# Two weight tiles trade slots, gate tiles alternate between two rings, and 17 instead of 15 gate/up tiles go by block products, in a hybrid decoder layer on one Trainium2 core

## Chip, cores and metric

The kernel runs on one core of a Trainium2 chip. The metric is the device time of the whole program in microseconds (us), lower is better. In the profile PE is TensorE's matmul and PEld its weight load, DVE is VectorE, ACT is ScalarE, POOL is GpSimd, SP is SyncE, which here only issues DMAs.

## What is computed

One decoder layer over 512 tokens of width 1024, cut from the reference:

```python
u = rms_norm(x, pre_mix_w)
proj = einsum('btd,de->bte', u, w_in)       # hg_q hg_f hg_i hg_g dn_q dn_k dn_v dn_g dn_a dn_b m_a m_b
o_a = head_rms_norm(hgrn2_mix(hg_q, hg_f, hg_i, lb)) * silu(hg_g)          # gated linear recurrence
o_b = head_rms_norm(gated_deltanet_mix(conv(dn_q, dn_k, dn_v), ...)) * silu(dn_g)
merged = sigmoid(m_a) * (o_a @ w_o_hg) + sigmoid(m_b) * (o_b @ w_o_dn)
h = x + rms_norm(merged @ w_out, post_mix_w)
gate, up = split(rms_norm(h, pre_ffn_w) @ w_gate_up)                        # 2 x 2816 columns
out = h + rms_norm((silu(gate) * up) @ w_down, post_ffn_w)
```

## The kernel before

Features lie on the 128 partitions and tokens in the free dimension. Every large product is made from three products of a high and a low part (`mm3`, lines 124 to 127): high by high (L126), low by high (L126), high by low (L127). `wload` (L109 to L122) brings a weight tile in with a DMA on SP's queue, makes its high part on ACT (L118) and its low part on DVE (L119). `dense_in` computes 128 output features of an input projection (called a dense tile here): 24 matmuls with 512 columns into one of three PSUM banks called `mm`, and then a function that empties the bank.

The order of the program's text is not the order on the engines: a scheduler places every instruction when the program is built. `high_priority` moves instructions ahead, `issue_after` holds one behind another, and a tile of a ring (a tag with so many buffers) can only be placed when the ring has a free buffer, in the order in which the program asks for them. On each engine the instructions then run in the built order. Three rings matter here: `dct` (9 buffers, L70), `hct` (7 buffers) and `out` (1 buffer, `spill`, L76).

Around the change the program does this:

- The DeltaNet mixer runs chunk by chunk (4 chunks of 128 tokens). While it runs, dense tiles fill TensorE.
- The sigmoid gates of the merge (`m_a`, `m_b`) that are computed early go out to DRAM. `gate_out` takes an `out` tile, applies the sigmoid with three ACT passes (L151 to L153), and issues a DMA on ACT's queue to `early_b` or `early_a`. It is used for the four tiles of `m_b0`, the four of `m_a0` and the first of `m_a1`. The program's text asks for the last two (the fourth of `m_a0` and the first of `m_a1`) just ahead of the HGRN2 mixer.
- The HGRN2 mixer (`hg_attn`, `hg_step`, `head_norm`) works on 4 chunks. For each chunk there are column sums, which need `dct` tiles that ACT and DVE split into two parts, six levels of a decay matrix on `hct` tiles (DVE, ACT, DVE, PE, DVE), and a step of the recurrent state. The dense tiles for `hg_g` (its last two), the DeltaNet output projection `y0`, `m_b1`, the fourth of `m_a0` and the first of `m_a1` lie ahead of it in the text. Their matmuls are listed in `dense`, and the mixer's matmuls are held behind every fifth of them (`self.marks`, `paced`). A mark is a lower bound only: it does not make a matmul run right behind it.
- Then `m_a1`'s other three tiles, the HGRN2 output projection `y1` (`merge`, 96 matmuls), and `out_proj`. The 16 half tiles of `w_out` come in through `dct` tiles and are split on ACT and on DVE or POOL (POOL for every odd `i`). Tiles 6 and 7 go to slots 13 and 6, in which until then the gates `self.ma[1]` and `self.ma[0]` lie.
- In `ffn` there are 22 gate/up tiles. A direct one costs 48 matmuls with 512 columns. The others go by block products (`winograd`): 7 products of 12 matmuls with 256 columns (L1109 to L1111), with more work on DVE and ACT for the weight combinations. Tiles 0 to 2 and each with `ft % 4 == 2` are direct.

## Time and profile before

| | us |
|---|---|
| three timed runs | 811.60, 815.22, 814.64 (median 814.64) |
| the profiled execution, its own time | 811.25 |
| its span, first to last instruction | 809.5 |

| engine | busy, share of the span |
|---|---|
| PE | 796.2 us, 98% |
| DVE | 591.7 us, 73% |
| ACT | 489.3 us, 60% |
| POOL | 75.4 us, 9% |

The profiled execution is 0.4% below the median of the timed runs. TensorE's granted clock was at its upper level for nearly the whole span (mean 0.999). Busy time of PE counts matmuls that overlap, so a busy PE says that PE had something in hand, not that it ran at its peak.

### The profile page before, as it was taken

The page shows a single profiled execution, that of the slowest core. Times are in us where ns is not written, and L with a number is a line of the kernel's source. Part 1 is how long each engine was busy: PE and PEld are TensorE (multiplying, and loading weights), DVE is VectorE, ACT ScalarE, POOL GpSimd, SP SyncE. Part 2 cuts the span into 40 slices and gives each one's busy share as a digit, 9 for nine tenths or more (in the row PEclk, how much of TensorE's full clock was granted, in tenths as well). Part 3 has the DMA queues.
Part 4 walks back from the last instruction along what each step waited for, and adds up shares of the span by engine and source line. Part 5 has one row for each costly group of instructions (what it writes and reads, how often), then busy time and mean ns, then how long its engine had stood idle before and what let it go on. Part 6 is the DMA issues. An engine that isn't in the chain of part 4 may idle for free.

```text
span 809.5 us, 12379 instructions
## 1 busy us (share of the span) xinstructions
PE 796.2 (98%) x4713; PEld 682.6 (84%) x4713; DVE 591.7 (73%) x961; ACT 489.3 (60%) x924; POOL 75.4 (9%) x113
## 2 busy tenths in 40 slices
PE   8999999999999999999999999999999999999996
PEld 8988888876888788888878899999999998888885
DVE  4794998513676888985775698887988888757773
ACT  6748888635687656657534454555556557556552
POOL 1000048610002000001310000000000000000000
PEclk9999999999999999999999999999999999999999
DMA  8525252552216212147621311414141416656731
GB/s 305 188 84 205 82 156 79 137 182 79 78 49 221 82 53 79 40 130 240 229 91 40 130 53 53 157 53 157 53 156 53 157 53 224 219 185 208 252 109 53
DMA packets 37852, 104.30 MB, mean 129 GB/s; under 512 B 4512, under 2 KB 4928, under 8 KB 37664
## 3 DMA queue, kind: packets, MB, share of 16 engines
q1 hardware_dynamic: 32688, 89.18, 32.7%
q0 software_dynamic: 3232, 10.93, 5.1%
q10 hardware_dynamic: 1872, 3.41, 1.2%
q8 instruction: 37, 0.61, 0.3%
q14 instruction: 23, 0.19, 0.1%
HBM read 94.83 MB, written 8.66 MB: 128 GB/s over the span
## 4 chain that ended last, share of the span: by engine, by line
PE 87%; DVE 4%; ACT 4%; DMA 3%; issue 1%; DVEq 0%; ACTq 0%; POOLq 0%
PE mm L126 23%; PE mm L127 11%; PE hps L126 3%; PE hps L1109 2%; PE hps L1110 2%; PE hps L1111 2%; PE dps L1226 2%; DVE s L156 2%; PE mm L1226 2%; PE mm L1225 2%; PE mm L1224 2%; PE dps L1224 2%; PE dps L1225 2%; DMA early_a<-out 2%; PE hps L699 2%; PE dps L1110 2%
## 5 line engine op out<-in xcount | busy, mean ns | idle before, releaser
L126 PE MATMUL mm<-s,whi 128*128 128x512 f32 (+1 forms) x976 | 304.1, 390 | 0.0
L126 PEld LDWEIGHTS mm<-s,whi 128*128 128x128 f32 x976 | 177.0, 188 | 32.9 <-ACT s L130 0.2
L127 PE MATMUL mm<-s,wlo 128*128 128x512 f32 (+1 forms) x488 | 188.5, 386 | 0.0
L119 DVE TENSOR_TENSOR wlo<-raw,whi 128x1024 fp32r<-128x1024 f32 x66 | 84.2, 1278 | 59.3 <-ACT whi L118 58.6
L127 PEld LDWEIGHTS mm<-s,wlo 128*128 128x128 f32 x488 | 91.7, 188 | 17.4 <-DVE wlo L119 0.6
L118 ACT CAST whi<-raw 128x1024 fp32r<-128x1024 f32 x66 | 69.2, 1049 | 40.8 <-PE mm L126 30.1
L119 DVE TENSOR_TENSOR wlo<-s,whi 128x1024 fp32r<-128x1024 f32 x40 | 48.9, 1223 | 15.0 <-ACT whi L118 14.6
L130 ACT CAST whi<-raw 128x512 fp32r<-128x512 f32 x60 | 36.8, 618 | 25.0 <-PE dps L1110 7.0
L1109 PE MATMUL hps<-s,whi 128*128 128x256 f32 x180 | 50.0, 278 | 0.7 <-DVE hct L156 0.4
L1111 PE MATMUL hps<-s,wlo 128*128 128x256 f32 x180 | 49.7, 276 | 0.0
L1110 PE MATMUL hps<-s,whi 128*128 128x256 f32 x180 | 49.7, 276 | 0.0
L130 ACT CAST whi<-s 128x512 fp32r<-128x512 f32 x45 | 27.9, 619 | 35.1 <-PE hps L1110 13.9
L156 DVE TENSOR_TENSOR s<-s,s 128x512 fp32r<-128x512 f32 (+3 forms) x59 | 43.0, 743 | 4.0 <-ACT s L130 1.9
L1214 ACT CAST hct<-s 128x256 fp32r<-128x256 f32 x44 | 17.6, 406 | 41.9 <-PE mm L1226 26.2
L118 ACT CAST whi<-s 128x1024 fp32r<-128x1024 f32 x40 | 41.9, 1048 | 1.4 <-PE dps L1110 1.4
L156 DVE TENSOR_TENSOR wlo<-raw,whi 128x512 fp32r<-128x512 f32 x60 | 40.5, 684 | 0.5 <-ACT whi L130 0.2
L130 ACT CAST s<-s 128x512 fp32r<-128x512 f32 (+2 forms) x36 | 23.7, 667 | 26.9 <-DVE s L156 20.0
L156 POOL TENSOR_TENSOR s<-s 128x126 f32<-128x126 f32 (+22 forms) x62 | 35.1, 565 | 9.9 <-DMA s<-scr 5.2
L126 PE MATMUL hps<-s,whi 128*128 128x512 f32 (+1 forms) x128 | 35.4, 363 | 0.0
L1109 PEld LDWEIGHTS hps<-s,whi 128*128 128x128 f32 x180 | 33.8, 188 | 1.4 <-DVE hct L156 0.7
L1110 PEld LDWEIGHTS hps<-s,whi 128*128 128x128 f32 x180 | 33.8, 188 | 0.1
L1111 PEld LDWEIGHTS hps<-s,wlo 128*128 128x128 f32 x180 | 33.8, 188 | 0.0
(313 smaller groups left out, 1868.4 us busy)
## 6 DMA issues: line engine op xcount, KB each, us to landing
raw<-in_w_in_a_dram SPq DMA_DIRECT2D x44, 512.0 KB, 3.4
s<-in_w_down_dram SPq DMA_DIRECT2D x44, 512.0 KB, 4.6
s<-in_w_gu_dram SPq DMA_DIRECT2D x60, 256.0 KB, 3.8
raw<-in_w_gu_dram SPq DMA_DIRECT2D x14, 512.0 KB, 3.4
raw<-in_w_o_dram SPq DMA_DIRECT2D x8, 512.0 KB, 4.8
dct<-in_w_out_dram SPq DMA_DIRECT2D x16, 256.0 KB, 6.9
s<-in_w_iab_dram SPq DMA_DIRECT2D x8, 260.0 KB, 6.5
s<-in_xT_dram SPq DMA_DIRECT2D x8, 256.0 KB, 6.8
```

The source lines that it names most:

```text
L118: nc.scalar.copy(hi[:, :n], raw[:, :n])
L119: nc.vector.tensor_tensor(out=lo[:, :n], in0=raw[:, :n], in1=hi[:, :n].bitcast(F32), op=ALU.subtract)
L126: return [mm(ps, lh, rh, start=start, stop=False), mm(ps, lh, rl, start=False, stop=False), mm(ps, ll, rh, start=False, stop=stop)]
L127: mm(ps, ll, rh, start=False, stop=stop)]
L130: self.nc.scalar.copy(hi, src)
L156: return (eng or self.nc.vector).tensor_tensor(out=out, in0=a, in1=b, op=op)
L1109: mm(ps, wh[:, k, :], ah[k], start=start and k == 0, stop=False, skip_group_check=True)
L1110: mm(ps, wh[:, k, :], al[k], start=False, stop=False, skip_group_check=True)
L1111: mm(ps, wl[:, k, :], ah[k], start=False, stop=k == 3, skip_group_check=True)
L1224: T.matmul(ps[:, n], gh, w[0][:, cols], start=st, stop=False, skip_group_check=True)
L1225: T.matmul(ps[:, n], gh, w[1][:, cols], start=False, stop=False, skip_group_check=True)
L1226: T.matmul(ps[:, n], gl, w[0][:, cols], start=False, stop=sp, skip_group_check=True)
```

## The change

Three edits. In `out_proj`, tile 6 of `w_out` goes to slot 6 and tile 7 to slot 13. In `mixers`, from the third tile of `m_b0` on `gate_out` gets its tiles by turns from `out` and from `dct`: the third tile of `m_b0` from `out`, its fourth from `dct`, the tiles of `m_a0` from `out`, `dct`, `out` and (its fourth) `dct`, and the first of `m_a1` from `out`. In `ffn`, the direct tiles are 0, 1, 2, 9 and 16 instead of 0, 1, 2, 6, 10, 14 and 18, so that 17 instead of 15 go by block products, in runs of six, six and five.

```diff
--- before.py
+++ after.py
@@ -1,4 +1,5 @@
 import math
+from itertools import cycle
 from contextlib import ExitStack, contextmanager, nullcontext
 
 import numpy as np
@@ -812,9 +813,9 @@
             self.stt(t, ps, self.hnw, t, ALU.mult, ALU.mult)
             nc.sync.dma_start(out=early_g[i], in_=t)
 
-        def gate_out(to):
+        def gate_out(to, tiles=self.spill):
             def f(ft, ps):
-                t = self.spill()
+                t = tiles()
                 self.sigmoid(t, ps)
                 A.dma_start(out=to[ft], in_=t)
             return f
@@ -841,8 +842,10 @@
             self.hg_prep((2, 3))
             early_e = {lev: self.hg_decay(0, lev) for lev in HG_LEVELS[:5]}
 
-        self.dense_in("m_b0", gate_out(early_b), fts=range(2, 4))
-        self.dense_in("m_a0", gate_out(early_a), fts=range(3))
+        two = cycle((self.spill, lambda: self.dct((P, 512))))
+        tiles = lambda: next(two)()
+        self.dense_in("m_b0", gate_out(early_b, tiles), fts=range(2, 4))
+        self.dense_in("m_a0", gate_out(early_a, tiles), fts=range(3))
         self.hq = self.slot(11, [P, NC_, NH, P])
         self.ghg = self.slot(12, [P, NH, S])
         for c in range(NC_):
@@ -868,8 +871,8 @@
             self.tt(y, ps, y, ALU.mult)
 
         self.dense_in("m_b1", gate_b)
-        self.dense_in("m_a0", gate_out(early_a), fts=(3,))
-        self.dense_in("m_a1", lambda ft, ps: gate_out(early_a)(4, ps), fts=(0,))
+        self.dense_in("m_a0", gate_out(early_a, tiles), fts=(3,))
+        self.dense_in("m_a1", lambda ft, ps: gate_out(early_a, tiles)(4, ps), fts=(0,))
         dense = self.log["hg_g"][48:] + self.log["y0"] + self.log["m_b1"] + self.log["m_a0"][72:] + self.log["m_a1"]
         self.marks = iter(dense[FIRST::PACE])
         at = []
@@ -943,7 +946,7 @@
                 j = (i % 2) * 2
                 h_, l_ = hi[:, j:j + 2, :], lo[:, j:j + 2, :]
             else:
-                w = self.slot((13, 6)[i - 6], [P, 2, 2, 512], F32R)
+                w = self.slot((6, 13)[i - 6], [P, 2, 2, 512], F32R)
                 h_, l_ = w[:, 0], w[:, 1]
             for j in range(2):
                 raw = self.dct((P, 512))
@@ -1173,7 +1176,7 @@
             pending = None
 
         for ft in range(NF):
-            if ft < 3 or ft % 4 == 2:
+            if ft < 3 or ft % 7 == 2:
                 for gu in range(2):
                     if (ft, gu) not in ws:
                         pss[ft, gu] = bank(gu)
```

The edits also move instructions that they do not name. Line numbers of the changed kernel are higher by one to three.

First place: ACT, around the first column sum of the HGRN2 mixer. `dct_2948` is the high part of that first column sum's operand, `mm_2487` the third tile of `m_a0`, `mm_2844` the last of `m_b1`, `mm_2879` the fourth of `m_a0`. Before:

```order
L130 CAST s_298_2067<-dct_2234 128x4x128
L118 CAST whi_2598<-raw_2597 128x1024
L151 ACTIVATE out_2512<-mm_2487 128x512
L130 CAST dct_2948<-dct_2946 128x512
L152 ACTIVATE out_2512<-out_2512,few 128x512
L153 ACTIVATE out_2512<-out_2512 128x512
L675 ACTIVATE dct_2956<-dct_2956 128x256
L819 DMA early_a<-out_2512 128x512
```

and with the change:

```order
L154 ACTIVATE mm_2844<-mm_2844 128x512
L119 CAST whi_3534<-raw_3533 128x1024
L152 ACTIVATE dct_2904<-mm_2879 128x512
L153 ACTIVATE dct_2904<-dct_2904,few 128x512
L131 CAST dct_2948<-dct_2946 128x512
L154 ACTIVATE dct_2904<-dct_2904 128x512
L820 DMA early_a<-dct_2904 128x512
L676 ACTIVATE dct_2956<-dct_2956 128x256
```

The cast of `dct_2948` stood behind the first sigmoid pass of the third tile of `m_a0`; now it stands behind the first two passes of the fourth, after all of `hg_g`, `y0` and `m_b1`.

Second place: PE, the last two levels of the mixer's last chunk (`hps_3438` and `hps_3450`). `mm_2879` is the fourth tile of `m_a0`; `dps_3460` and `dps_3487` are the column sums of the mixer's last two head norms. Before:

```order
L699 MATMUL hps_3438<-hct_3432 128x128 x4
L126 MATMUL mm_2879<-s_62_563,whi_2874 128x512
L127 MATMUL mm_2879<-s_60_561,wlo_2875 128x512
L126 MATMUL mm_2879<-s_60_561,whi_2874 128x512
L126 MATMUL mm_2879<-s_62_563,whi_2874 128x512
L127 MATMUL mm_2879<-s_60_561,wlo_2875 128x512
L699 MATMUL hps_3450<-hct_3444 128x128 x4
L126 MATMUL mm_2879<-s_60_561,whi_2874 128x512
```

and with the change, up to the last row ahead of `y1`:

```order
L700 MATMUL hps_3414<-hct_3408 128x128
L700 MATMUL hps_3426<-hct_3420 128x128 x4
L392 MATMUL dps_3460<-dct_3456,onesr 128x512
L700 MATMUL hps_3438<-hct_3432 128x128 x4
L393 MATMUL dps_3460<-dct_3457,onesr 128x512
L700 MATMUL hps_3450<-hct_3444 128x128 x4
L712 MATMUL dps_3468<-hct_3317,s_25_185 128x128 x4
L735 MATMUL dps_3468<-s_380_2517,st_3399 128x128 x4
L392 MATMUL dps_3487<-dct_3483,onesr 128x512
L393 MATMUL dps_3487<-dct_3484,onesr 128x512
```

Before, five dense matmuls stood between two levels; now the levels, the state's step and both head norms follow each other with no dense matmul between them. With the change all dense tiles up to the fourth of `m_a0` (264 matmuls from the third of `hg_g` on) and half of the first of `m_a1` stand ahead of the mixer's first matmul, and only the other half and `m_a1`'s remaining three tiles stand within the mixer, all of them in its first two chunks and at the head of its third.

Third place: the DMA queue of SP, around the first loads of `w_out`. Before:

```order
L987 DMA hct_3909<-in_x_dram 128x512
L117 DMA raw_3567<-in_w_in_a_dram 128x1024
L117 DMA raw_3605<-in_w_o_dram 128x1024
L950 DMA dct_3775<-in_w_out_dram 128x512
L950 DMA dct_3779<-in_w_out_dram 128x512
L950 DMA dct_3783<-in_w_out_dram 128x512
L950 DMA dct_3787<-in_w_out_dram 128x512
```

and with the change:

```order
L118 DMA raw_3645<-in_w_o_dram 128x1024
L118 DMA raw_3685<-in_w_o_dram 128x1024
L118 DMA raw_3725<-in_w_o_dram 128x1024
L118 DMA raw_4203<-in_w_gu_dram 128x1024
L990 DMA hct_3908<-in_x_dram 128x512
L990 DMA hct_3909<-in_x_dram 128x512
L953 DMA dct_3775<-in_w_out_dram 128x512
L953 DMA dct_3779<-in_w_out_dram 128x512
```

The first load of `w_out` stood behind the first load of `w_o`, and further loads of `w_o` came between the later ones; now all four loads of `w_o`, one of `w_gu` and two of `x` stand ahead of all sixteen.

## Rows read from the trace of the kernel before

**Rows 1.** The page's part 1: busy time of each engine.

```profile
PE 796.2 (98%) x4713; PEld 682.6 (84%) x4713; DVE 591.7 (73%) x961; ACT 489.3 (60%) x924; POOL 75.4 (9%) x113
```

**Rows 2.** Waits of PE: who waited for whom, us in total, times, longest.

```profile
PE hps L391 <- ACT dct L130: 1.7, 1, 1.7
PE mm L961 <- ACT s L130: 1.5, 1, 1.5
...
PE mm L962 <- DVE s L156: 0.2, 1, 0.2
```

**Rows 3.** Windows: stretch, its length, then busy us of each engine.

```profile
core 0: us, PE busy (x) PEld busy (x) DVE busy (x) ACT busy (x) POOL busy (x), PEclk, DMA share, GB/s
266.00:372.50 106.50, 104.72 (x619) 86.11 (x618) 89.60 (x163) 66.97 (x140) 2.20 (x4) 1.00 0.25 77
389.45:411.23 21.78, 21.78 (x98) 18.02 (x96) 19.69 (x23) 12.13 (x19) 7.22 (x5) 1.00 0.43 145
494.02:682.63 188.61, 187.92 (x1454) 179.20 (x1452) 159.82 (x278) 108.13 (x199) 0.00 (x0) 1.00 0.34 110
503.56:513.08 9.52, 9.52 (x86) 9.52 (x85) 8.72 (x17) 5.44 (x11) 0.00 (x0) 1.00 0.34 112
```

**Rows 4.** The chain that ended last, 255 to 269: start, us, what.

```profile
255.72 6.10 DMA early_a<-out
...
264.75 2.01 DMA early_a<-out
...
268.00 0.50 PE hps L391
```

**Rows 5.** Timeline of PE, third `hg_g` tile: start, us, instruction, count [idle before].

```profile
264.15 0.61 PE L126 MATMUL mm<-s,whi 128*128 128x512 f32 x2
264.60 0.39 PE L127 MATMUL mm<-s,wlo 128*128 128x512 f32 x1
264.83 0.61 PE L126 MATMUL mm<-s,whi 128*128 128x512 f32 x2
```

**Rows 6.** Groups of DVE from 266 to 372.5.

```profile
L156 DVE TENSOR_TENSOR hct<-hct,s 128x256 f32<-128x256 f32 x43 | 16.1, 417 | 2.6 <-ACT hct L656 2.6
L119 DVE TENSOR_TENSOR wlo<-raw,whi 128x1024 fp32r<-128x1024 f32 x12 | 14.6, 1218 | 2.3 <-ACT whi L118 1.7 <-PE dps L734 0.6
...
L156 DVE TENSOR_TENSOR s<-mm,s 128x512 f32<-128x512 f32 x8 | 5.5, 690 | 1.2 <-ACT mm L153 1.0 <-PE mm L127 0.2
...
L159 DVE SCALAR_TENSOR_TENSOR s<-mm,few,s 128x512 f32<-128x512 f32 x2 | 1.5, 750 | 0.3 <-ACT s L153 0.3
```

**Rows 7.** Timeline of ACT: the last head norm, and one sigmoid of three passes.

```profile
367.58 0.59 ACT L606 ACTIVATE dct<-dps 128x512 f32<-128x512 f32 x1
...
371.33 0.63 ACT L612 ACTIVATE dct<-dct 128x512 f32<-128x512 f32 x1
...
381.04 0.59 ACT L151 ACTIVATE s<-mm 128x512 f32<-128x512 f32 x1
...
382.04 0.73 ACT L152 ACTIVATE s<-s,few 128x512 f32<-128x512 f32 x1
...
383.17 0.63 ACT L153 ACTIVATE s<-s 128x512 f32<-128x512 f32 x1
```

**Rows 8.** Timeline of DVE and of POOL while `w_out` is split.

```profile
391.34 4.56 DVE L119 TENSOR_TENSOR wlo<-raw,whi 128x1024 fp32r<-128x1024 f32 x2
...
399.84 1.22 DVE L119 TENSOR_TENSOR wlo<-raw,whi 128x1024 fp32r<-128x1024 f32 x1
...
390.81 4.00 POOL L156 TENSOR_TENSOR s<-dct,s 128x512 fp32r<-128x512 f32 x2 [0.56 <-ACT s L130]
```

**Rows 9.** The tile `in_w_out_dram`: its 16 DMAs, issue to landing.

```profile
DMA to landing us min/median/max: 4.4/6.9/8.8
```

**Rows 10.** Timeline of PE in block products: two groups of three matmuls.

```profile
499.48 0.28 PE L1109 MATMUL hps<-s,whi 128*128 128x256 f32 x1
...
499.82 0.28 PE L1109 MATMUL hps<-s,whi 128*128 128x256 f32 x1
```

**Rows 11.** Windows at the end, columns as in group 3; PEclk is the granted clock.

```profile
803.00:804.00 1.00, 0.36 (x4) 0.16 (x2) 0.82 (x3) 0.14 (x1) 0.00 (x0) 1.00 0.00 0
...
807.00:808.00 1.00, 0.00 (x0) 0.00 (x0) 0.00 (x0) 0.00 (x0) 0.00 (x0) 0.93 1.00 346
808.00:809.50 1.50, 0.00 (x0) 0.00 (x0) 0.00 (x0) 0.00 (x0) 0.00 (x0) 0.50 0.05 15
```

## The prediction

> **What bounds the kernel now.** I read the busy times first: PE has something in hand for 796.2 of 809.5 us, DVE for 591.7 [rows 1]. Then what PE waits for: one wait of 1.7 us at the first column sum of the HGRN2 mixer and two of 1.5 and 0.2 us at the first matmuls of the output projection are all that matters in the middle [rows 2]. So PE's own stream sets the time, and an edit can gain only by taking matmuls out or by ending one of these few waits. It can lose much more: what PE hides (the vector work of the mixer) becomes visible if the matmuls that hide it go elsewhere. Three matmuls with 512 columns take 0.68 us from start to start (264.15 to 264.83), so 0.227 us each [rows 5]; three with 256 columns in a block product take 0.34 us (499.48 to 499.82) [rows 10].
>
> **Block products for two more tiles.** A direct gate/up tile is 48 x 0.227 = 10.9 us of PE, a block-product tile 84 x 0.1133 = 9.5 us. Two more of them save 2 x 1.36 = 2.7 us. DVE is the risk: in a stretch of the length of one such tile it is busy 8.72 of 9.52 us (the last row of its group) [rows 3], and runs of three tiles become runs of six with one direct tile between. A run of three has not slowed PE much (in the whole stretch PE misses 0.7 of 188.6 us) and DVE was busy 159.8 us there [rows 3], to which two tiles add about 2 x (8.7 - 4) = 9 us, 4 us being my estimate for a direct tile's two 1.2 us low parts [rows 6] and three gate products of 0.6 to 0.7 us like the group of s<-mm [rows 6]; that is 169 of 186 us. Bounds for the loss: nothing, and all of the 2.7 us. I take 0.1, so **-2.6 us**.
>
> **Gate tiles from two rings: ACT's waits.** Before, ACT's second gate waits for the landing of the first one's DMA, 6.1 and then 2.0 us, and the first column sum stands behind it [rows 4]: that is PE's 1.7 us [rows 2]. The second ring ends these waits; the gates' own DMAs stay as many and as large, on ACT's queue as before. But the dct ring is handed out in the order in which the program asks. The fourth gate of m_a0 now asks for a dct tile just ahead of the mixer's first dct tile, so the mixer can't have its tiles before that gate is made. The order on ACT shows it: the cast of dct_2948, the first operand of the mixer, now stands behind two passes of the sigmoid over mm_2879. On each engine instructions run as listed, so PE's order follows: 264 dense matmuls that lay between the mixer's matmuls run first, and the mixer is left with those of four tiles.
>
> **What the mixer then costs.** I compare the time at which PE can start y1, which needs all chunks of the mixer.
> Before: y1 starts at 389.45, since its 96 matmuls of 0.227 us fill the 21.78 us up to 411.23 [rows 3].
> After: the third tile of hg_g starts at 264.15 [rows 5]; 264 x 0.227 = 59.9 us later, at 324.0, PE is done with the fourth of m_a0. What follows is bound by DVE. In 266 to 372.5 DVE is busy 89.6 us [rows 3]; off go the 12 weight low parts of 14.6 us and the evacuations of y0, m_b1 and hg_g of 5.5 and 1.5 us [rows 6], which leaves 68.0 us for the mixer. Five products of 0.42 us of the first chunk [rows 6] can be made ahead, and five low parts of 1.22 us fall into this part (by the changed order of DVE): 68.0 - 2.1 + 6.1 = 72 us. PE has only the tile after the gate's, three more, and the mixer's own matmuls in the meantime: 96 x 0.227 = 21.8 us, and 389.45 - 264.15 - 1.7 - 360 x 0.227 = 41.9 us as they stood before; 64 us in sum, less than DVE's 72.
> DVE does not run without waits. If it never waited, y1 would start at 324 + 72 = 396, 6.5 us late. If it were busy as in the stretch before, 89.6 of 106.5 or 84% [rows 3], 72 would become 85.6, and y1 would start at 409.6, 20 us late. I take the upper part. The end is a chain with little for DVE: ACT has three sigmoids of three passes (m_a1's gates, whose slot the mixer holds until its last level), about 3 x 1.8 us [rows 7], and behind them the last head norm, whose squares start at 367.58 and whose last exponential ends at 371.96 before [rows 7], then a product and a cast, about 5.7 us: 11 us with some 5.5 us of DVE work. The head is paced by PE: 8.4 us with 7 us of DVE work until the second column sum. Between them lie 59.5 us of DVE work; with 6% of waits (my choice) 63.4. So 324 + 8.4 + 63.4 + 11 = 406.8, **+17.4 us**, in which the 1.7 us are already credited.
>
> **Slots of w_out and the late loads.** Before, PE waits 1.5 and 0.2 us for a part of w_out [rows 2] that lay in slot 13 and so had to wait for the last gate. Slot 6 comes free earlier, so the swap gains up to these 1.7 us. Against it stands the order on SP's queue: the loads of w_out now come behind y1's and two of x, whose tiles come from the mixer's last levels, and their dct tiles from its last head norms, so most of the 16 land after y1 has started (4.4 to 8.8 us each [rows 9]). Their splits then meet y1's evacuations. In the 21.78 us of y1 DVE was busy 19.69 us before [rows 3], with half of the splits already done. And while POOL splits w_out, DVE is slower: two low parts took 4.56 us beside POOL, one alone 1.22 us [rows 8].
> The Trainium skill (GPSIMD Engine Reference, 1. Specifications) says that GpSimd's SBUF interfaces are shared with VectorE, and that they contend when a DVE instruction has two SBUF inputs. The rows agree; were DVE left alone by POOL, the term would be the gain of 1.7 us and the sum below 824.3 instead of 828.0.
> Bounds: -1.7 (all hidden) and +6 us: some 10 us of w_out's and y1's splits by DVE at twice their time, less 4 us of cover by the first 18 matmuls of the projection. I take **+2 us**.
>
> **The sum**: 17.4 + 2 - 2.6 = +16.8 us on the profiled execution's 811.25, 828.0. The timed runs lie 0.35 to 4 us above it (median 814.64), so I add 2 us: **830 us**.
>
> **Rivals.**
> A, faster: the new PE order costs nothing, since the mixer's DVE work hides all the same. Then only the gains count: -1.7 - 1.7 - 2.7 = -6.1 us, about 807. For this DVE's 72 us would have to fit into PE's 64 us with no wait, and the chain at the end would have to vanish. It decides below some 62 us of DVE work. Nothing in the rows brings 10 us less. For it speaks only that PE was never seen to wait for the mixer's levels, but then five dense matmuls lay between two of them. 4%.
> B, the clock falls. In the mixer's last two chunks PE now has about half of 41.9 us of work in some 40 us. At the end of the span PE's last work ends at 803.36, the granted clock is 0.93 on the mean of 807 to 808 and 0.50 from there on [rows 11]: half, the lower of its two levels (1.2 and 2.4 GHz). If PE's gaps in the mixer do the same, the mixer's matmuls double; most hide under DVE (+3 us), but four steps of the chain at the end do not (0.9 + 0.9 + 0.5 us, so +2.3), and y1's first matmuls run slowly too (+2): +7, about 837.
> The Trainium skill (TensorE: Matmul & The Clock Gate, Part 1) says that the array's clock is halved by default and that activity releases it. By that rule a thin stretch can fall back, as the end of the trace does after its last matmul; no row here has a thin stretch in the middle. 15%.
> C, DVE waits more: the static order was laid out with PE full, and each level goes DVE, ACT, DVE, PE, DVE. At 75% busy the 72 us become 96, y1 starts at 420, and with 6 us from w_out the sum is 811.25 + 30.6 + 6 - 2.6 + 2 = 847. 12%.
> D, no difference: the mixer costs what the three edits gain, about 6 us, so 813. It needs a DVE without any wait. 3%.
> The forecast, by itself 819 to 840, has the other 66%.
>
> **How the numbers follow.** A change of 0.5% (4 us) is about what the runs can tell from none. Faster by more holds A, 4%; within it D, 3%; slower the rest, 93%. The range begins at the lower bound of the mixer's cost with a w_out term of nothing, 811.25 + 6.5 - 2.6 + 2 = 817, and reaches to C's 847: 818 to 846 leaves out A, D and about half of C, some 13%.
>
> **What would show it.** PE's waits, 3.4 us in the three rows before, would become 15 to 30 us between the first column sum (now near 327 instead of 268) and y1 (now near 407 instead of 389), named after DVE and ACT of the mixer; DVE there above 85%. PE's first wait of 1.7 us is gone, ACT's 6.1 us behind the DMA too. The projection's wait moves from the cast of tile 6 to a low part or an evacuation of y1. Gate/up takes 186 instead of 188.6 us. The prediction is wrong if y1 starts before 398, if the clock falls in the middle, or if gate/up does not get shorter.

## The result, and the profile after

The changed kernel takes 840.53 us (median of four runs, 838.21 to 844.53), the kernel before 813.9 us beside it: a ratio of 1.034, with an interval of 1.029 to 1.038. It is some 27 us slower. The forecast was some 17 us more, 830 us in all, in a range of 818 to 846. The profiled execution took 844.53 us, span 842.7, and was the slowest of the four.

Part 1 of the page of the changed kernel answers to [rows 1]. PE is busy for 17.5 us more, though two more block-product tiles were to take work off it; DVE for 4.7 us more.

```profile
PE 813.7 (97%) x4785; PEld 699.8 (83%) x4785; DVE 596.4 (71%) x989; ACT 494.2 (59%) x938; POOL 74.9 (9%) x113
```

The waits of PE in the changed kernel (columns as in [rows 2]). The wait at the first column sum and those at the output projection are gone. In their place stand waits for vector and scalar work of the mixer (`hps` and `dps` are its banks), and one of 2.8 us at the first matmul of y1.

```profile
PE hps L700 <- DVE hct L157: 5.2, 4, 1.7
PE hps L392 <- ACT dct L131: 4.5, 3, 2.4
PE mm L127 <- ACT s L131: 2.8, 1, 2.8
```

The timeline of PE in the changed kernel, at the start of the third `hg_g` tile, at the mixer's first column sum and at the first matmul of y1 (columns as in [rows 5]):

```profile
267.16 0.62 PE L127 MATMUL mm<-s,whi 128*128 128x512 f32 x2
...
329.84 0.50 PE L392 MATMUL hps<-dct,onesr 128*128 128x512 f32 x1
...
423.94 0.79 PE L127 MATMUL mm<-s,whi 128*128 128x512 f32 x1 [2.82 <-ACT s L131]
```

Before, the tile started at 264.15, the column sum 3.85 us later at 268.00, and y1 at 389.45 [rows 3 to 5]. Now the column sum comes 62.7 us after the tile, and y1 156.8 us after it instead of 125.3.

The windows of the changed kernel, by stage (columns as in [rows 3]): the 264 dense matmuls from the third `hg_g` tile on; the mixer in two parts; y1; the projection; gate/up.

```profile
267.16:327.00 59.84, 59.84 (x266) 49.56 (x264) 23.99 (x29) 27.12 (x39) 0.78 (x1) 1.00 0.40 130
327.00:371.30 44.30, 41.50 (x251) 32.74 (x249) 36.59 (x67) 26.62 (x59) 0.00 (x0) 1.00 0.21 62
371.30:423.94 52.64, 37.36 (x187) 30.43 (x187) 36.01 (x76) 28.33 (x64) 3.45 (x6) 0.66 0.29 95
423.94:448.37 24.43, 24.43 (x97) 19.94 (x98) 20.39 (x28) 13.19 (x22) 8.59 (x6) 0.89 0.44 148
448.37:528.89 80.52, 80.09 (x441) 69.35 (x440) 53.92 (x88) 37.03 (x86) 3.64 (x4) 1.00 0.22 72
528.89:715.48 186.59, 185.50 (x1526) 180.52 (x1524) 170.80 (x306) 111.34 (x213) 0.00 (x0) 1.00 0.34 111
```

In the first row DVE has 24.0 us of work in 59.8 us, while PE is full; in the next two it has 72.6 us in 96.9 us, while PE waits. In the mixer's second half the granted clock is 0.66 on the mean. Two windows of the same trace show how it falls:

```profile
367.90:371.31 3.41, 0.77 (x2) 0.37 (x2) 3.27 (x7) 3.38 (x10) 0.00 (x0) 1.00 0.16 34
371.31:378.10 6.79, 6.33 (x38) 5.02 (x39) 4.31 (x11) 3.43 (x9) 0.00 (x0) 0.50 0.18 63
```

PE works for 0.77 of 3.41 us, and from 371.31 on the clock is at the lower of its two levels (1.2 and 2.4 GHz); it changes level several times until y1 has run for 5.4 us. The Trainium skill (TensorE: Matmul & The Clock Gate, Part 1) says that the clock is halved by default and released by activity; the trace agrees, with 0.50 behind a thin stretch in the middle of the kernel.

### The profile page after: what moved, and what is told of

The parts are those of the page before. It is cut to its first block, busy times and chain, and to the rows that moved or that the text cites. A ratio compares the mean times of both kernels' runs of the same rounds, so it can differ in the third digit from the quotient of the medians.

```text
span 842.7 us, 12584 instructions
## 1 busy us (share of the span) xinstructions
PE 813.7 (97%) x4785; PEld 699.8 (83%) x4785; DVE 596.4 (71%) x989; ACT 494.2 (59%) x938; POOL 74.9 (9%) x113
## 3 DMA queue, kind: packets, MB, share of 16 engines
q10 hardware_dynamic: 1872, 3.41, 1.2%
## 4 chain that ended last, share of the span: by engine, by line
PE 91%; DVE 6%; ACT 2%; issue 1%; DMA 0%; DVEq 0%; ACTq 0%; POOLq 0%
PE mm L127 25%; PE mm L128 12%; PE hps L1112 2%; PE hps L1113 2%; PE hps L1114 2%; PE hps L127 2%; PE hps L700 2%; PE dps L1113 2%; PE dps L1229 2%; PE mm L1228 2%; PE mm L1227 2%; PE mm L1229 2%; PE dps L1112 2%; PE dps L1228 2%; PE dps L1227 2%; PE dps L1114 2%
## 5 line engine op out<-in xcount | busy, mean ns | idle before, releaser
L127 PE MATMUL mm<-s,whi 128*128 128x512 f32 (+1 forms) x944 | 292.5, 390 | 2.8 <-ACT s L131 2.8
L128 PE MATMUL mm<-s,wlo 128*128 128x512 f32 (+1 forms) x472 | 181.8, 385 | 0.0
L120 DVE TENSOR_TENSOR wlo<-raw,whi 128x1024 fp32r<-128x1024 f32 x62 | 76.4, 1232 | 85.9 <-ACT whi L119 85.9
L1112 PE MATMUL hps<-s,whi 128*128 128x256 f32 x204 | 57.0, 279 | 1.1 <-DVE hct L157 0.4
L1114 PE MATMUL hps<-s,wlo 128*128 128x256 f32 x204 | 56.4, 276 | 0.0
L1113 PE MATMUL hps<-s,whi 128*128 128x256 f32 x204 | 56.4, 276 | 0.0
L131 ACT CAST whi<-raw 128x512 fp32r<-128x512 f32 x68 | 41.7, 618 | 19.8 <-PE dps L1113 7.9
L157 DVE TENSOR_TENSOR wlo<-raw,whi 128x512 fp32r<-128x512 f32 x68 | 45.9, 685 | 0.8 <-ACT whi L131 0.3
L1217 ACT CAST hct<-s 128x256 fp32r<-128x256 f32 x44 | 17.6, 406 | 41.8 <-PE mm L1229 26.2
L1112 PEld LDWEIGHTS hps<-s,whi 128*128 128x128 f32 x204 | 38.3, 188 | 2.3 <-DVE hct L157 1.7
L1113 PEld LDWEIGHTS hps<-s,whi 128*128 128x128 f32 x204 | 38.3, 188 | 0.1
L1112 PE MATMUL mm<-s,whi 128*128 128x256 f32 x136 | 37.6, 276 | 0.0
L1114 PE MATMUL mm<-s,wlo 128*128 128x256 f32 x136 | 37.6, 276 | 0.0
L1113 PE MATMUL mm<-s,whi 128*128 128x256 f32 x136 | 37.5, 276 | 0.0
```

The lines of the kernel that those rows point to most:

```text
L120: nc.vector.tensor_tensor(out=lo[:, :n], in0=raw[:, :n], in1=hi[:, :n].bitcast(F32), op=ALU.subtract)
L127: return [mm(ps, lh, rh, start=start, stop=False), mm(ps, lh, rl, start=False, stop=False), mm(ps, ll, rh, start=False, stop=stop)]
L128: mm(ps, ll, rh, start=False, stop=stop)]
L131: self.nc.scalar.copy(hi, src)
L157: return (eng or self.nc.vector).tensor_tensor(out=out, in0=a, in1=b, op=op)
L1112: mm(ps, wh[:, k, :], ah[k], start=start and k == 0, stop=False, skip_group_check=True)
```

## The experiments

Theory 1: the loss comes from the gate tiles alone, and there from one request: the gate that asks for a `dct` tile last ahead of the mixer pushes the mixer behind 264 dense matmuls. Theory 2: the mixer cost 14 us more than I forecast because the clock fell in its thin half. Theory 3: its length is set by the amount of DVE's work. The rivals stand in the expectations: the tile's kind and not the order of requests, the slots of `w_out`, and a chain through DVE, ACT and PE in which DVE has slack and the clock only follows.

Each was timed beside the kernel before, on one chip with the others of its group. There were three groups: the slots and block products, the gate tiles, the last two gates back and four constants; the changed kernel again, the later dct tile, the gates asked for later and two constants; DVE's work and one constant. To compare places in time I use the distance from the start of the third `hg_g` tile to the start of y1 (125.3 us before, 156.8 in the changed kernel), here called **the mixer's stretch**. Each is that of one profiled execution. The columns of all windows are those of [rows 3].

An edit can move instructions that it does not name. Read off the traces, the order of PE's, DVE's and ACT's instructions in the mixer's stretch is the same in both executions of the changed kernel and in the kernel with the gate tiles alone. It is another one in all the other kernels below, so a small difference in their stretch is not the edit's alone.

**The changed kernel again** (no edit), as a second execution to compare with:

> The changed kernel once more, beside the other kernels of this group. Its profiled execution of the result lost 3 us at the start to a clock that came up late, and was the slowest of four. Expected: 25 to 29 us slower than before, y1 154 to 157 us after the third tile of hg_g starts (125.3 before), the granted clock 0.65 to 0.8 in the mixer's second half.

Measured: 841.21 us, ratio 1.0345 (1.0327 to 1.0364); the profiled execution took 840.77. Its windows: the mixer's stretch, y1, the projection, gate/up; then three parts of the mixer, from the end of the 264 matmuls to the second column sum, to ACT's three last sigmoids, and to y1; and the thin part from 366 us on.

```profile
263.93:420.32 156.39, 137.46 (x701) 111.77 (x699) 96.56 (x170) 82.43 (x161) 4.23 (x7) 0.90 0.29 99
420.32:444.53 24.21, 24.21 (x97) 19.79 (x97) 20.43 (x28) 13.33 (x22) 8.61 (x6) 0.90 0.45 148
444.53:525.06 80.53, 80.10 (x441) 69.34 (x440) 53.95 (x88) 37.15 (x86) 3.64 (x4) 1.00 0.22 72
525.06:711.79 186.73, 185.62 (x1525) 180.64 (x1524) 170.72 (x306) 111.56 (x213) 0.00 (x0) 1.00 0.33 111
...
323.77:332.69 8.92, 8.92 (x39) 6.79 (x38) 5.92 (x10) 6.87 (x13) 0.00 (x0) 1.00 0.25 88
332.69:407.85 75.16, 61.88 (x373) 49.79 (x372) 60.97 (x123) 38.66 (x93) 1.62 (x3) 0.84 0.15 50
407.85:420.32 12.47, 6.82 (x26) 5.64 (x26) 5.67 (x10) 9.71 (x19) 1.84 (x3) 0.64 0.76 261
...
366.00:420.32 54.32, 36.60 (x188) 29.67 (x187) 37.87 (x79) 30.61 (x71) 3.45 (x6) 0.70 0.28 94
```

The third `hg_g` tile starts at 263.93 here, as before the change, and at 267.16 in the first profile: the 3 us at the start belonged to that one execution. In it PE ran at about half the pace there, 28 matmuls in the 6.20 us from 6.71 on against 53 in the 6.60 us from 6.31 on before. The column of the granted clock reads 1.00 in both, so the late clock that the expectation names is inferred from the pace. All the stages behind it repeat.

**The slots and the block products alone,** as an edit of the kernel before:

```diff
-                w = self.slot((13, 6)[i - 6], [P, 2, 2, 512], F32R)
+                w = self.slot((6, 13)[i - 6], [P, 2, 2, 512], F32R)
...
-            if ft < 3 or ft % 4 == 2:
+            if ft < 3 or ft % 7 == 2:
```

> The kernel before with the slot swap of w_out and the two further block-product tiles, without the new gate tiles. Theory 1 (all of the loss comes from the gate tiles): 3 to 4 us faster than before, since gate/up gains 2.0 us as in the changed kernel and PE's waits of 1.5 and 0.2 us for w_out go. Rival (the swap costs by late loads of w_out and by POOL beside DVE, my +2 of the prediction): the stretch from y1 to the output projection is longer and the sum is 1 us faster to 2 us slower.

Measured: 807.53 us, ratio 0.9934 (0.9910 to 0.9957). That is 6.1 us faster than the median beside it; the stages account for about 5. The mixer's stretch, the projection and gate/up in its windows:

```profile
263.33:387.71 124.38, 123.49 (x702) 101.66 (x701) 99.12 (x172) 80.80 (x163) 7.49 (x10) 1.00 0.34 117
...
409.47:490.08 80.61, 80.22 (x442) 69.38 (x440) 55.57 (x90) 37.76 (x87) 3.63 (x4) 1.00 0.22 72
490.08:676.87 186.79, 185.68 (x1526) 180.70 (x1524) 171.17 (x306) 111.28 (x213) 0.00 (x0) 1.00 0.33 111
```

The projection takes 80.6 instead of 82.8 us, gate/up 186.8 instead of 188.6; both edits gain, and the rival falls. The mixer's stretch is 0.9 us shorter too: PE's wait at the first column sum, 1.7 us before [rows 2], is 0.8 us here. Why, I did not follow.

**The gate tiles alone,** as an edit of the kernel before:

```diff
+        two = cycle((self.spill, lambda: self.dct((P, 512))))
+        tiles = lambda: next(two)()
...
-        self.dense_in("m_a0", gate_out(early_a), fts=(3,))
+        self.dense_in("m_a0", gate_out(early_a, tiles), fts=(3,))
```

(and the same at the other three calls.)

> The kernel before with the alternating gate tiles alone. Theory 1: the whole loss and a little more, 28 to 36 us slower than before (845 us), the first column sum of the mixer near 327 us, y1 near 420 us, the clock at half in parts of the mixer's second half. Rival (the three edits only cost together, w_out's order with the bare mixer): less than 20 us slower.

Measured: 842.82 us, ratio 1.0369 (1.0341 to 1.0396), 29.2 us slower: the whole loss and a little more. The mixer's stretch, and the thin part from 366 us on:

```profile
263.48:417.99 154.51, 135.34 (x701) 109.40 (x699) 96.53 (x170) 82.04 (x161) 4.22 (x7) 0.92 0.30 101
...
366.00:417.99 51.99, 34.40 (x187) 27.29 (x187) 37.41 (x79) 29.92 (x70) 3.44 (x6) 0.75 0.30 100
```

The stretch is 1.9 us shorter than in the second execution (156.39), with the same instructions in the same order. Up to 112 us into it ACT's instructions start within 0.2 us of each other in the two traces. The clock had fallen in both by then; here it is back at its upper level at 374.97, 111.5 us into the stretch, there at 377.45, 113.5 us into it. From there on this kernel gains. So the clock by itself moves y1: 0.75 instead of 0.70 in the thin part is worth these 1.9 us.

**The last two gates back in the one `out` tile:**

```diff
-        self.dense_in("m_a0", gate_out(early_a, tiles), fts=(3,))
-        self.dense_in("m_a1", lambda ft, ps: gate_out(early_a, tiles)(4, ps), fts=(0,))
+        self.dense_in("m_a0", gate_out(early_a), fts=(3,))
+        self.dense_in("m_a1", lambda ft, ps: gate_out(early_a)(4, ps), fts=(0,))
```

> The changed kernel, but the last two gates (the fourth of m_a0 and the first of m_a1) take the one out tile as before; the five gates ahead of them still alternate. Theory 1 (the request of the m_a0 gate for a dct tile ahead of the mixer's first one is what pushes the mixer behind 264 dense matmuls): the first column sum stands again among the hg_g tiles near 270 us, y1 starts near 390 us, no half clock in the middle, and the kernel is 3 to 7 us faster than before (807 to 811 us). Rival (any gate in dct tiles starves the mixer, since seven of nine tiles are left while their DMAs run): y1 starts at 400 us or later and the kernel is 10 us or more slower than before.

Measured: 806.04 us, ratio 0.9915 (0.9894 to 0.9937): 7.6 us faster than before, the fastest kernel of this study, though not told apart from the one without any new gate tile (0.9910 to 0.9957). The mixer's first column sum in its timeline, and the mixer's stretch in its windows:

```profile
271.13 0.50 PE L392 MATMUL hps<-dct,onesr 128*128 128x512 f32 x1
```

```profile
263.62:386.72 123.10, 123.10 (x701) 100.30 (x700) 97.73 (x173) 80.83 (x163) 6.69 (x9) 1.00 0.37 127
```

Of the five gates that alternate, two still have a `dct` tile, and PE does not wait at all in the stretch. So a `dct` tile for a gate costs nothing by its kind here; the loss hangs on the last two requests.

**The dct tile one gate later:**

```diff
-        self.dense_in("m_a0", gate_out(early_a, tiles), fts=(3,))
+        self.dense_in("m_a0", gate_out(early_a), fts=(3,))
```

> The changed kernel with one more edit: the fourth gate of m_a0 takes the out tile, and the next one, the first of m_a1, takes the dct tile in its place. Theory 1 (whichever gate asks for a dct tile last ahead of the mixer holds the mixer back until its matmuls are done): the mixer starts 24 matmuls, 5.4 us, later than in the changed kernel; y1 starts 3 to 6 us later and the kernel is slower by that. Rival (the dct ring is short by a tile while the gate's DMA runs, wherever the gate stands): the same time as the changed kernel, within 2 us.

Measured: 841.03 us, ratio 1.0355 (1.0306 to 1.0404), the same as the changed kernel. The first column sum in the timeline, and the mixer's stretch:

```profile
331.89 0.50 PE L392 MATMUL hps<-dct,onesr 128*128 128x512 f32 x1
```

```profile
263.77:420.80 157.03, 136.10 (x702) 110.03 (x700) 96.19 (x170) 82.03 (x161) 4.24 (x7) 0.91 0.30 98
```

The start moved as theory 1 says: 68.1 us behind the tile instead of 62.7. The end did not: 157.0 us, so theory 1's 3 to 6 us more in time did not come. The time is the one that the rival named, but the rival has no reason for the later column sum. From the first column sum to y1 the mixer took 88.9 us, where it took 93.7 in the second execution, and DVE stood idle in them for 19.2 us (88.91 less 69.72) instead of 22.4 (93.70 less 71.31). Why it waited less is not settled: the order on all three engines is another one behind the first column sum, and from 366 us on the clock is at 0.76 instead of 0.70.

**The two gates asked for behind chunk 0 of the mixer:**

```diff
-        self.dense_in("m_a0", gate_out(early_a, tiles), fts=(3,))
-        self.dense_in("m_a1", lambda ft, ps: gate_out(early_a, tiles)(4, ps), fts=(0,))
...
             run(self.hg_attn(0, at, early_e))
+        self.dense_in("m_a0", gate_out(early_a, tiles), fts=(3,))
+        self.dense_in("m_a1", lambda ft, ps: gate_out(early_a, tiles)(4, ps), fts=(0,))
```

(The list of marks is built as it is needed, since the last dense tiles are now logged later.)

> The changed kernel, but the program asks for the fourth gate of m_a0 and the first of m_a1 after chunk 0 of the mixer instead of ahead of it; the kinds of their tiles stay (dct, then out). Theory 1 (order of requests): chunk 0 runs again among the tiles of hg_g, first column sum 4 to 8 us after the third of them starts (62.7 in the changed kernel); chunks 1 to 3 still stand behind the gate, so y1 starts 129 to 138 us after that tile (125.3 before, 154.5 to 156.8 in the changed kernel), and the kernel is 2 us faster to 10 us slower than before. Rival (a gate in a dct tile costs by its kind): within 4 us of the changed kernel.

Measured: 834.55 us, ratio 1.0259 (1.0234 to 1.0284). The first column sum, and the mixer's stretch with its parts up to the end of the 264 matmuls and behind them:

```profile
271.80 0.50 PE L392 MATMUL hps<-dct,onesr 128*128 128x512 f32 x1
```

```profile
264.28:411.94 147.66, 130.97 (x702) 105.65 (x700) 96.12 (x170) 80.82 (x161) 4.22 (x7) 0.94 0.31 104
264.28:333.02 68.74, 68.59 (x334) 56.13 (x332) 31.86 (x44) 29.49 (x47) 0.78 (x1) 1.00 0.33 113
333.02:411.94 78.92, 62.38 (x370) 49.53 (x368) 64.26 (x126) 51.33 (x115) 3.44 (x6) 0.89 0.29 97
```

The kinds of tile are unchanged; only the place of the two gates in the program's text moved, with their matmuls and weight loads. The first column sum is back at 7.5 us behind the tile: theory 1 holds, and the rival, within 4 us of the changed kernel, falls. My size was off: y1 starts 147.7 us behind the tile, not 129 to 138. I had counted chunk 0 as a quarter of the mixer, but it brings DVE only 7.9 us of work ahead of the end of the 264 matmuls (31.86 us there instead of 24.0), and behind them DVE is left with 64.3 us instead of 72.6 (5.92 + 60.97 + 5.67 in the second execution). The 264 matmuls take 68.7 us instead of 59.8, since chunk 0's stand among them, and what lies behind them takes 78.9 us instead of 96.6. That is 17.6 us less for 8.3 us less of DVE's work; the rest of it these runs do not explain.

**More and less work for DVE.** In the mixer's last two chunks one operation of each level is doubled, with the same result, or one is left out, which gives another output:

```diff
-        self.tt(w(E), w(self.hf[:, c]), ref, ALU.subtract)
+        for _ in range(2 if c >= 2 else 1):
+            self.tt(w(E), w(self.hf[:, c]), ref, ALU.subtract)
```

```diff
-        self.tt(Ev[:, :, 0, :], Ev[:, :, 0, :], kv[:, :, 0, :], ALU.mult)
+        if c < 2:
+            self.tt(Ev[:, :, 0, :], Ev[:, :, 0, :], kv[:, :, 0, :], ALU.mult)
```

> The changed kernel; in the mixer's last two chunks the first vector operation of each of six levels (the difference of 128 x 512 at the head of hg_decay) is done twice, with the same result: 12 more DVE instructions of 0.6 us, 7.2 us. Theory 3 (DVE's amount of work sets the mixer's length, as my forecast had it: 72 us of work, few waits): y1 starts 6 to 8 us later, 162 us or more after the third tile of hg_g (156.4 and 156.8 without). Rival (DVE has slack in the bare mixer, 72.7 us of work in 97 us, and the chain through ACT and PE sets the length): at most 3 us later, below 160 us.

> The changed kernel; in the mixer's last two chunks the second vector operation of each level, the product with the keys (128 x 256 out, 0.34 us), is left out, so the output is another one: 12 DVE instructions, 4.1 us less. Theory 3 (DVE's amount of work sets the length): y1 starts 4 us or more earlier, 152.5 us or less after the third tile of hg_g. Rival (chain): only what lies in the chain goes, 0 to 2.5 us.

Measured: 851.59 us, ratio 1.0486 (1.0465 to 1.0506), and 834.67 us, ratio 1.0277 (1.0258 to 1.0296). The mixer's stretch and its thin part with more work:

```profile
264.28:431.57 167.29, 142.47 (x702) 116.00 (x700) 103.89 (x182) 82.26 (x161) 4.22 (x7) 0.84 0.28 93
366.00:431.57 65.57, 41.88 (x189) 34.05 (x189) 45.59 (x91) 30.95 (x73) 3.44 (x6) 0.59 0.24 78
```

and with less:

```profile
263.95:413.63 149.68, 130.87 (x701) 107.54 (x700) 92.61 (x158) 81.75 (x161) 4.22 (x7) 0.92 0.31 105
366.00:413.63 47.63, 30.03 (x188) 25.42 (x188) 33.99 (x67) 30.12 (x72) 3.45 (x6) 0.76 0.33 109
```

DVE is busy for 7.3 us more, and y1 starts 10.9 us later than in the second execution; 4.0 us less, and 6.7 us earlier. The rival, with 3 and 2.5 us at most, falls: although DVE stands idle for a quarter of the mixer, the idle time is no slack that could take the added work. It comes between operations that wait for each other.

Two things are not shown. One is the size for each microsecond of work, which was above theory 3's 6 to 8 us. The clock moves along (0.59 and 0.76, against 0.70 in the second execution from 366 us on), and the order moved: with less work ACT is done with `m_a1`'s three sigmoids at 395.8, ahead of a head norm between whose passes they stand in the changed kernel. The other is whether the amount of DVE's work sets the length, as theory 3 has it, or its place. Both operations stand in each level's own chain of DVE, ACT and PE, so a chain in which DVE has no slack would show the same.

**Matmuls of constants that keep PE at work.** At 14 places in the last two chunks (six levels and one output in each), ahead of the place's own matmuls and into the same bank; their results are not used. The edit with four, one of its places shown:

```diff
             with self.paced():
+                self.fill(c, ps)
                 for h in range(NH):
                     T.matmul(ps[:, h, :], E[:, h, :], E[:, h, :], start=True, stop=True)
...
+    def fill(self, c, ps):
+        for _ in range(4 if c >= 2 else 0):
+            self.nc.tensor.matmul(ps, self.onesr, self.onesr.unsqueeze(1).to_broadcast([P, NH, P]), start=True, stop=True)
```

> The changed kernel with four matmuls of constants (512 columns, results overwritten, so extra work that the reference doesn't need) ahead of the matmuls of each level, and of the output, of the mixer's last two chunks; some 15 places, 14 us of PE work at the full clock. Theory 2 (the clock's fall in the thin second half makes up the 14 us by which the mixer cost more than I forecast): the granted clock stays above 0.9 there, y1 starts 5 us or more earlier than in the changed kernel (424 less its late start), its first matmuls run at 1.0, and the kernel is 4 to 12 us faster than the changed one. Rival (the static chain DVE, ACT, PE, DVE with its waits sets the time, the clock follows from it): y1 starts within 2 us of the changed kernel's or later, by up to 14 us.

> As the kernel with four matmuls of constants at each place of the mixer's last two chunks, but with two: half the extra work (7 us of PE, overwritten, not needed by the reference). With four the clock held at 0.9 to 1.0, but the extra matmuls themselves stood in the chain. Theory 2 (the clock costs 5 us or more): the clock stays above 0.9 and y1 starts 150 us or less after the third tile of hg_g (152.4 with four, 154.5 to 156.8 without). Rival (the chain of DVE, ACT and PE sets the time at either clock): 152 us or more, whatever the clock.

> As the kernels with four and two matmuls of constants at each place of the mixer's last two chunks, with one (3.4 us of PE, overwritten): less extra work in the chain, less to hold the clock. Those two started y1 152.4 and 152.1 us after the third tile of hg_g, the changed kernel 156.4 and 156.8. If the clock is worth more than these 4.4 us and the extra matmuls ate the rest, and if one still holds the clock above 0.9, it is 151 us or less; if the clock falls as in the changed kernel, 154 us or more; 152 to 153 with a clock above 0.9 says that the clock is worth some 4 us and no more.

Measured, with four, two and one: 837.52, 836.82 and 836.81 us; ratios 1.0301 (1.0268 to 1.0333), 1.0288 (1.0260 to 1.0316) and 1.0309 (1.0291 to 1.0327). The mixer's stretch of each, with four, then its thin part:

```profile
265.27:417.65 152.38, 140.75 (x758) 113.67 (x756) 96.62 (x170) 82.18 (x161) 4.23 (x7) 0.98 0.31 103
366.00:417.65 51.65, 40.19 (x245) 31.77 (x245) 39.28 (x81) 31.84 (x74) 3.45 (x6) 0.95 0.32 102
```

with two:

```profile
264.62:416.76 152.14, 137.65 (x729) 110.32 (x727) 96.55 (x170) 81.81 (x161) 4.25 (x7) 0.94 0.31 102
366.00:416.76 50.76, 37.12 (x216) 28.42 (x216) 38.58 (x80) 30.68 (x74) 3.47 (x6) 0.83 0.30 101
```

and with one:

```profile
263.85:416.79 152.94, 137.73 (x715) 110.18 (x713) 96.42 (x170) 82.19 (x161) 4.23 (x7) 0.94 0.30 101
366.00:416.79 50.79, 36.78 (x202) 27.94 (x200) 37.68 (x79) 30.40 (x71) 3.46 (x6) 0.81 0.31 100
```

More work on PE makes the kernel faster, by 4.4 us with two, which ran in one group with the changed kernel (841.21). From 366 us on the granted clock is at 0.81, 0.83 and 0.95 with one, two and four, instead of 0.70, and the stretch is 152.9, 152.1 and 152.4 us long instead of 156.4. Theory 2 had asked for more: 5 us or more with four, 150 us or less with two, and the upper level at y1's first matmuls. With four y1 still takes 24.13 us:

```profile
417.65:441.78 24.13, 24.13 (x96) 19.80 (x97) 20.40 (x28) 13.20 (x22) 8.59 (x6) 0.90 0.43 142
```

The 14 us that theory 2 wanted are not there: with the clock at 0.95 DVE still does 39.3 us of work in 51.7.

But the 4 us need not be the clock's alone, since the extra matmuls also changed the order. In the changed kernel the three sigmoids of `m_a1`'s gates (from L152 on) stand behind a head norm's pass at L612; with one, two and four they stand ahead of it. The timeline of ACT in the second execution, then with two:

```profile
407.22 0.69 ACT L612 ACTIVATE dct<-dps,few 128x512 f32<-128x512 f32 x1 [0.71 <-PE dps L393]
407.85 1.58 ACT L152 ACTIVATE s<-mm 128x512 f32<-128x512 f32 x3
```

```profile
403.43 1.58 ACT L152 ACTIVATE s<-mm 128x512 f32<-128x512 f32 x3 [0.79 <-DVE hct L157]
...
408.28 0.69 ACT L612 ACTIVATE dct<-dps,few 128x512 f32<-128x512 f32 x1
```

The extra matmuls also stand ahead of needed ones and cost time themselves. These runs do not part the clock, the order and that cost. That the clock is a cause is shown by the kernel with the gate tiles alone, at 1.9 us. An estimate from it: the clock was at the lower level for 26.0 of 51.99 us there and for 32.6 of 54.32 us in the second execution (means of 0.75 and 0.70), so 6.6 us less of it gave 1.9 us. If every microsecond at the lower level cost as much, all 32.6 would cost some 9 us; no run shows that.

## Why the prediction was right in kind and short in size

By stages, in us against before (forecast; the first profile; the second execution):

| step | forecast | first | second |
|---|---|---|---|
| start, to the third `hg_g` tile | 0 | +3.0 | -0.2 |
| mixer, to y1 | +17.4 | +31.5 | +31.1 |
| y1 | 0 | +2.7 | +2.4 |
| projection to gate/up | +2 | -2.3 | -2.3 |
| gate/up | -2.6 | -2.0 | -1.9 |
| down and end | 0 | +0.4 | +0.4 |
| sum | +16.8 | +33.3 | +29.5 |

The sums meet the times of the profiled executions: 811.25 + 33.3 = 844.5, 811.25 + 29.5 = 840.8.

**The gate's tile** did what the prediction says. PE is done with the 264 matmuls at 327.0, 59.84 us after the third tile starts (forecast 59.9), and the first column sum stands behind them. Two runs show the cause: the same gates with the last two in the `out` tile, and the same tiles asked for later, both bring the column sum back. ACT's waits for the gates' DMAs went too, as forecast; they had been 2.9 us in three waits, and the 6.1 and 2.0 us of the prediction are the DMAs' own times [rows 4].

**What the mixer then costs** is the term that was mis-sized, and the step in it is "with 6% of waits (my choice) 63.4". Head and DVE's work were right: 8.92 us against 8.4, and 72.6 us of DVE work against 72, of which 60.97 in the middle part against 59.5. But that part took 75.16 us, not 63.4: DVE waited there for 14.2 us, 19%, most of it for ACT's exponentials (L657) and for PE's products of the state (L728) and of the levels (L700). The waits of DVE in that part of the second execution, the longest first:

```profile
DVE hct L157 <- ACT hct L657: 4.0, 2, 2.5
DVE st L160 <- PE dps L728: 3.3, 2, 1.8
DVE hct L701 <- PE hps L700: 3.3, 5, 1.2
```

The end took 12.47 us instead of 11. The rows had a somewhat better figure: 84% busy in the stretch before, which I named and then left for a choice of fewer waits. It would have given 20 us, still 11 too few; it was read while PE was full. Rival C, with DVE busy for 75%, had +30.6 us for this term; measured are 31.1, with DVE busy for 72.6 of 96.6 us, which is 75%. Only its 6 us for `w_out` were not there.

**The clock fell too**, as rival B has it. Its price was 7 us, some 5 in the mixer and 2 in y1. Measured are 2.4 to 2.7 us in y1, 24.21 and 24.43 us instead of 21.78 [rows 3]. In the mixer the same order took 1.9 us less where the clock was lower for a shorter time, so it costs at least that. B and C came together and not one in place of the other: the bare mixer leaves PE thin, the clock falls, and DVE waits for ACT and PE. How the 13.7 us beyond the forecast (31.1 less 17.4) divide between the clock and the waits that the chain has at any clock stays open.

**The slots of `w_out`** had the wrong sign, +2 against -2.3. The waits of 1.5 and 0.2 us went, and nothing took their place. SP's queue issues all sixteen loads from 407.40 on, in 24.66 us, so the first stand 16 us ahead of y1, in the mixer's thin end, and they land after 3.4 us (median) instead of 6.9 [rows 9]:

```profile
407.40 24.66 SPq L953 DMA_DIRECT2D dct<-in_w_out_dram x16
...
DMA to landing us min/median/max: 2.8/3.4/5.5
```

The collision that I feared is there, in the timelines of DVE and POOL:

```profile
435.68 3.49 DVE L157 TENSOR_TENSOR s<-s,s 128x512 fp32r<-128x512 f32 x3
...
434.94 3.08 POOL L157 TENSOR_TENSOR s<-dct,s 128x512 fp32r<-128x512 f32 x2 [4.42 <-ACT s L131]
```

Three operations that took 0.6 to 0.7 us each elsewhere in y1 took 3.49 us together here. But PE is busy for all of y1's 24.43 us, and the projection does not wait. That the loads came early enough for the splits, which my +2 left out, fits these rows and was not tested. The swap itself can be told from the kernel with the gate tiles alone, which has the bare mixer and the old slots. Its projection takes 1.5 us longer than the 80.53 of the second execution:

```profile
442.13:524.14 82.01, 80.70 (x442) 69.27 (x440) 55.81 (x91) 37.03 (x86) 1.11 (x2) 1.00 0.21 71
```

**Block products** gained 2.0 and 1.9 us of the forecast 2.6. PE's gaps in gate/up grew from 0.69 [rows 3] to 1.09 us, where I had 0.1 for the longer runs, and its busy time fell by 2.4 us, not 2.7.

**The prediction's own signs, and luck.** It called itself wrong if the clock falls in the middle, and the clock did. Its other two signs held: y1 did not start before 398, and gate/up got shorter. PE waits for 18.1 us of the 94.1 between the first column sum and y1, within the 15 to 30 named, but DVE is busy for 75% there and not for more than 85%, and the projection's wait did not move to another place, it is gone. The measured 840.5 us lie inside the range because that took in half of rival C; the forecast by itself reached to 840. In part this was luck: the wrong sign for `w_out` took 4.3 us off a sum that was short by 13.7 us in the mixer and 2.4 us in y1.

## What to carry to other kernels

A tile taken from a ring is also a place in a queue of requests: before a temporary is moved to a ring that a later stage uses, look at who asks next, and whether that one then waits for the slow owner. Work that is hidden behind a full engine costs its own chain when it is laid bare; a share of waits read while another engine was full is too small for the bare stretch (here 84% busy became 75%), and the thinned engine's clock can fall with it. An engine that idles for a quarter of a stretch can still set its length: add and remove a known amount of its work, and see how much of it comes out at the end. Before a size is taken from such an edit, compare the order of all other instructions in the two traces; here only one of the variants had kept it.

## What was unexpected of the hardware

Extra matmuls without any use made the kernel some 4 us faster: 14 matmuls of 512 columns, one at each place, came with a mean granted clock of 0.81 instead of 0.70 from 366 us to y1 and with a stretch that is 3.5 us shorter, though the order of ACT's and DVE's instructions changed with them. The same instructions in the same order took 154.5 us in one kernel and 156.4 in another, at 0.75 and 0.70. And the loss outlives the thin stretch: PE has work in hand for all of y1, and its first 5.4 us still run at the lower level (2.4 to 2.7 us).
